# Prompt attention of a hybrid decoder step: score tiles of 1024 columns in place of 512

## The chip, the cores and the metric

The kernel runs on one NeuronCore of a Trainium2 chip. The metric is the device time of one execution in microseconds; the median of three runs before the change is 3355.91 us. The engines of the core that matter here are TensorE (PE in the profile, its weight loads PEld), VectorE (DVE), ScalarE (ACT) and GpSimd (POOL). Each of them works through its own queue in order.

## The reference, cut to what matters

The whole computation is one inference step of a one-layer decoder: an input projection, forgetting attention over a prompt of 2048 tokens with 8 heads of 64, an mLSTM over the same prompt, attention of 8 sample sequences over paged caches of 8192 keys each, an output projection with layer norm and an MLP with layer norm. The change lies in the attention over the prompt:

```python
SEQ, FOX_HEADS, FOX_HEAD_DIM, Q_BLOCK = 2048, 8, 64, 128

def _fox_prompt(q, k, v, logf):
    L = jnp.cumsum(logf, axis=1).transpose(0, 2, 1)
    ...
    def block(args):
        q_i, L_i, i = args
        s = jnp.einsum('bqhd,bkhd->bhqk', q_i, k).astype(jnp.float32) * scale
        s = s + L_i[..., :, None] - L[:, :, None, :]
        q_pos = i * Q_BLOCK + jnp.arange(Q_BLOCK)
        s = jnp.where(k_pos[None, :] <= q_pos[:, None], s, -jnp.inf)
        p = jax.nn.softmax(s, axis=-1)
        return jnp.einsum('bhqk,bkhd->bqhd', p.astype(v.dtype), v)
```

A row of scores belongs to one query. The mask is causal, so the 128 queries of row tile `qt` (0 to 15) see `(qt + 1) * 128` keys.

## The kernel before, in words

The kernel is one stream of instructions in program order, which a scheduler turns, at compile time, into one order for each engine. An instruction that comes earlier in the program goes first when its operands and its buffers are there; where they are not, a later one may pass it in the order that is compiled. On the chip the orders are fixed, and semaphores hold each engine until what it needs is done. A tile of a pool has a number of buffers (`bufs`); a new one can be written when the last reader of the tile that had its buffer before is through.

The stages are: input projections with the mLSTM beside them and the first part of the sample attention between them (up to about 940 us of the profiled span), the attention over the prompt (`phase_b`, about 940 to 1378 us), and then the output projection, the MLP and the rest of the sample attention, interleaved.

In `phase_b` the work is cut into 64 units, `units = [(h, g) ...]`: head `h` from 0 to 7, and within it `g` from 0 to 7. Unit `g` covers two row tiles of 128 queries, `qt = 2g` (called A below) and `qt = 2g + 1` (called B). The loop at the end of `phase_b` writes `scores` of unit n, then now and then `keys` and `queries` for what comes next, then `values` of unit n - 1 (`LA = 1`).

`scores(z, g)`: for A and then for B, the keys are taken in blocks of up to 512. Two matmuls (L1046 and L1047, query high part and low part) put a block of scores into a PSUM tile `pS`; there are three such banks, two of the stage's own and one that is shared. VectorE then adds the forget values (L1053; L1057 for the 128 columns at the diagonal, with the mask in `nd`), writes the sum into an SBUF tile `S` and keeps the row maximum of the block in `mx`. L1060 reduces these to the negative row maximum. `S` has 10 buffers of 512 columns of fp32.

`values(z, g, sc)`: for A and B, ScalarE takes the exponential of each `S` tile in place, with the row maximum as bias, and leaves the row sum of the tile in a column of `lp` (L1072: an ACTIVATE and then a read of the accumulator). L1073 adds up the columns of `lp`. Then, for chunks of four key blocks of 128 (`k0` = 0, 4, 8, 12) and in each for A and then B, TensorE transposes four 128x128 blocks of `S` into a PSUM tile `pt` of three buffers (L1085), ScalarE (L1088) or VectorE (L1090, for B's even chunks) copies it to `PT`, and TensorE multiplies the chunk with the values (L1094) into `po`. The chunks are called A0, B0, A1, B1, A2, B2, A3, B3 below. An `S` tile of 512 columns is read for the last time by the transposes of its one chunk.

At the end of a unit L1100 and L1102 move `po` to `ot`, and each fourth unit `finish` scales by the row sums and stores. `keys` (L1002, L149, L152) and `queries` (L149, L152) prepare the operands of the matmuls; `split_hi` (L149) and `split_lo` (L152) are helpers used all over the kernel.

Of the kernel before, what the change touches and what calls it, by code (L numbers as in the profile page):

```python
# [10 lines left out]
F32 = mybir.dt.float32  # L11
# [14 lines left out]
S = 2048  # L26
# [26 lines left out]
def body(ctx, tc, I, O, stages):  # L53
    nc = tc.nc
    V, A, G, T, SY = nc.vector, nc.scalar, nc.gpsimd, nc.tensor, nc.sync
# [20 lines left out]
    ident = cst.tile([128, 128], F32, name="ident")  # L76
# [52 lines left out]
    def tick(us):  # L129

        macc[0] += us
        while macc[1] and macc[0] > macc[2]:
            macc[0] -= macc[2]
            if beside(macc[1][0]) == 0:
                macc[1].pop(0)
        if not macc[1]:
            macc[0] = 0.0
        acc[0] += us
        while acc[1] is not None and acc[0] > acc[2]:
            acc[0] -= acc[2]  # L140
            attend()
# [809 lines left out]
    def phase_b():  # L951
        es = ExitStack()
        pb = es.enter_context(tc.tile_pool(name="pb", bufs=1, reuse_waits="tile"))
# [6 lines left out]
        def bank():  # L960

            turn[0] += 1
            if turn[0] % 3 == 0:
                return pps.tile([128, 512], F32, name="pS", tag="sX", bufs=1)
            return ppb.tile([128, 512], F32, name="pS", bufs=2)
# [61 lines left out]
        def scores(z, g):  # L1027

            qh, ql = z.pop(("q", g))
            ks = z["ks"]  # L1030
            forget = lambda a, b: Bz["nl"][:, a:b] if z["h"] == 0 and a < 512 else z["nl"][:, a:b]
            out = []
            for i in range(2):
                qt = 2 * g + i
                n = (qt + 1) * 128
                qs = slice(i * 128, i * 128 + 128)
                mx = pb.tile([128, 8], F32, name="mx", bufs=8)
                nd = pb.tile([128, 128], F32, name="nd", bufs=3)
                lastnd[0] = G.tensor_tensor(nd, forget(qt * 128, n), dmask, op=OP.add)
                st = []  # L1040
                j = 0
                for a in range(0, n, 512):
                    b = min(n, a + 512)
                    w = max(b - a, 256)
                    pS = bank()
                    T.matmul(pS[:, :w], qh[:, qs], ks[:, a:a + w], start=True, stop=False)  # L1046
                    last["PE"] = T.matmul(pS[:, :w], ql[:, qs], ks[:, a:a + w], start=False, stop=True)  # L1047
                    tick(0.42)
                    sp = pb.tile([128, 512], F32, name="S", bufs=10)
                    st.append(sp)  # L1050
                    e = min(b, qt * 128)
                    if e > a:
                        last["DVE"] = V.tensor_tensor_reduce(out=sp[:, :e - a], in0=pS[:, :e - a], in1=forget(a, e), scale=1.0, scalar=NEG,  # L1053
                                               op0=OP.add, op1=OP.max, accum_out=mx[:, j:j + 1])
                        j += 1
                    if b == n:
                        V.tensor_tensor_reduce(out=sp[:, e - a:b - a], in0=pS[:, e - a:b - a], in1=nd, scale=1.0, scalar=NEG,  # L1057
                                               op0=OP.add, op1=OP.max, accum_out=mx[:, j:j + 1])
                        j += 1
                V.tensor_reduce(mx[:, 7:8], mx[:, :j], axis=AX.X, op=OP.max, negate=True)  # L1060
                out.append((st, mx))
            return out

        def values(z, g, sc):

            for i, (st, mx) in enumerate(sc):
                qt = 2 * g + i
                n = (qt + 1) * 128
                lp = pb.tile([128, 4], F32, name="lp", bufs=8)
                for k, sp in enumerate(st):  # L1070
                    w = min(512, n - k * 512)
                    last["ACT"] = A.activation(sp[:, :w], sp[:, :w], AF.Exp, bias=mx[:, 7:8], accum_out=lp[:, k:k + 1])  # L1072
                V.tensor_reduce(z["ls"][:, qt:qt + 1], lp[:, :len(st)], axis=AX.X, op=OP.add)  # L1073

            po = ppb.tile([128, 256], F32, name="po", bufs=1)
            nk = 2 * g + 2
            for k0 in range(0, nk, 4):
                PT = pb.tile([128, 4, 256], F32, name="PT", bufs=4)
                for i in range(2):
                    kk = min(4, 2 * g + i + 1 - k0)  # L1080
                    if kk <= 0:
                        continue
                    pt = ppb.tile([128, 4, 128], F32, name="pt", bufs=3)
                    for k in range(kk):
                        T.transpose(pt[:, k], sc[i][0][k0 // 4][:, k * 128:(k + 1) * 128], ident)  # L1085
                    dst = PT[:, :kk, i * 128:i * 128 + 128]
                    if i == 0 or (k0 // 4) % 2 != 0:
                        A.copy(dst, pt[:, :kk])  # L1088
                    else:
                        V.tensor_copy(dst, pt[:, :kk])  # L1090
                for k in range(k0, min(k0 + 4, nk)):
                    q0 = 128 if k == nk - 1 else 0
                    c = (k % 2) * 64
                    last["PE"] = T.matmul(po[c:c + 64, q0:], z["vn"][:, k], PT[:, k - k0, q0:],  # L1094
                                          start=(k < 2), stop=(k >= nk - 2), skip_group_check=True)
                tick(0.45 * min(4, nk - k0))
            if g % 4 == 0:
                z["ot"] = pb.tile([64, 1024], F32, name="ot", bufs=2)
            od = z["ot"][:, (g % 4) * 256:(g % 4) * 256 + 256]
            A.copy(od, po[0:64])  # L1100
            q0 = 128 if g == 0 else 0
            V.tensor_tensor(od[:, q0:], od[:, q0:], po[64:128, q0:], op=OP.add)  # L1102
            if g % 4 == 3:
                finish(z, g // 4)

        def finish(z, half):

            h, ls, ot = z["h"], z["ls"], z["ot"]
            lr = pb.tile([128, 32], F32, name="lr", bufs=2)
            V.reciprocal(lr, ls)  # L1110
            lt = pb.tile([128, 32], F32, name="lt", bufs=2)
            V.transpose(lt, lr)
            o = half * 1024
            for a in range(4):
                SY.dma_start(drl[h, o:o + 1024].rearrange("(t a q) -> a t q", a=4, q=32)[a], lt[a * 32 + half * 8:a * 32 + half * 8 + 8])
            for q in range(2):
                rl = pb.tile([64, 512], F32, name="rl", bufs=2)
                SY.dma_start(rl, dap(drl, h * S + o + q * 512, [[0, 64], [1, 512]]))
                s = slice(q * 512, (q + 1) * 512)
                G.tensor_tensor(ot[:, s], ot[:, s], rl, op=OP.mult)  # L1120
                SY.dma_start(dmix[h // 2, (h % 2) * 64:(h % 2) * 64 + 64, o + q * 512:o + q * 512 + 512], ot[:, s])
# [12 lines left out]
        sc = {}  # L1134
        LA = 1
        for n in range(len(units) + LA):
            if 10 <= n < 16 and acc[1] is not None:

                with tc.issue_after(lastnd[0].ins):
                    attend()  # L1140
            if n == 12:
                wo.extend(half_wo(0, q) for q in range(4))
            if n < len(units):
                h, g = units[n]
                sc[n] = scores(Z[h], g)
                if h == 0 and g % 2 == 0 and g < 6:
                    keys(Z[0], g // 2 + 1)
                if h < 7:
                    if g == 3:
                        Z[h + 1] = head(h + 1)  # L1150
                        forget_values(Z[h + 1], 0, S)
                    if g >= 4:
                        keys(Z[h + 1], g - 4)
                if n + 1 < len(units):
                    queries(Z[units[n + 1][0]], units[n + 1][1])
            if n >= LA:
                h, g = units[n - LA]
                values(Z[h], g, sc.pop(n - LA))
# [698 lines left out]
```

## Time and profile before

| what | value |
|---|---|
| median of 3 runs | 3355.91 us (3352.63 to 3362.21) |
| profiled execution: span from first to last instruction | 3381.2 us (no other time is listed for it) |
| instructions | 57759 |
| mean granted TensorE clock | 0.988 of full speed |
| busy: PE, PEld | 3266.7 us (97%), 2623.4 us (78%) |
| busy: DVE, ACT, POOL | 2145.9 us (63%), 1413.8 us (42%), 869.5 us (26%) |
| attention over the prompt: exponentials, first and last start | 320, from 940.0 us to 1372.4 us |

How to read it: a busy share over the whole span is a mean over stages with different limits, so the stage from 940 to 1378 us is asked for by itself. A busy PE is not PE at its peak, because matmuls are pipelined and their ends are modelled; the waits of PE and of its weight loads say more. In a row of a group of instructions stand the line, the engine, the operation, the tiles written and read, the shape, the count, then the busy time and the mean length of one in ns, then the time that the engine stood idle just before them and what ended it. In a row of the timeline stand the start in us, the length in us, the engine, the line and the operation; several like instructions in a row are one row with their count.

### The profile page before, as it was taken

To read this page: it belongs to the slowest core of one execution; us is meant where nothing else is said; L and a number is where in the kernel's file an instruction comes from. 1 tells how busy PE (TensorE), PEld (TensorE's weight loads), DVE (VectorE), ACT (ScalarE), POOL (GpSimd) and SP (SyncE) were. 2 spreads that over 40 slices of the span, in tenths; PEclk is the share of its full clock that TensorE was granted. 3 is DMA by queue.
4 is the path that set the end of the run, shared out by engine and by line. 5 is a ranking of instruction groups with operands and counts; after the bars stand their busy time and mean duration, and the time that the engine had idled before them with its cause. 6 is when DMAs were issued, how large, how long until landed. Compare 5 with 4: busy or idle time off the path is not lost. (4 is left out here: it accounts for less than half of the span.)

```text
span 3381.2 us, 57759 instructions
## 1 busy us (share of the span) xinstructions
PE 3266.7 (97%) x21564; PEld 2623.4 (78%) x21564; DVE 2145.9 (63%) x5180; ACT 1413.8 (42%) x2989; POOL 869.5 (26%) x928
## 2 busy tenths in 40 slices
PE   9999999999999999999999999999999999999998
PEld 8998897787866667677777776777777777888886
DVE  5857567556478878655666667666676545644545
ACT  4444245334378888422332333232332323433332
POOL 0112122422332222365423324323243110100001
PEclk9999999999999999999999999999999999999999
DMA  5665765866652322587776768767678545532221
GB/s 172 165 189 179 221 206 180 292 212 219 227 166 81 90 76 61 209 283 245 286 249 244 247 226 299 254 234 270 209 258 289 198 164 160 168 103 83 87 76 66
DMA packets 427232, 646.25 MB, mean 191 GB/s; under 512 B 83148, under 2 KB 320016, under 8 KB 426056
## 3 DMA queue, kind: packets, MB, share of 16 engines
q1 hardware_dynamic: 350184, 363.22, 35.3%
q0 software_dynamic: 74304, 270.57, 21.8%
q10 hardware_dynamic: 2464, 8.78, 0.7%
q8 instruction: 170, 2.79, 0.3%
q14 instruction: 110, 0.90, 0.1%
HBM read 589.63 MB, written 52.83 MB: 190 GB/s over the span
## 5 line engine op out<-in xcount | busy, mean ns | idle before, releaser
L1422 DVE TENSOR_TENSOR y<-y,py 128x512 f32<-128x512 f32 (+1 forms) x475 | 320.5, 681 | 310.7 <-PE py L159 287.4
L149 ACT ACTIVATE wh<-wr 128x1024 fp32r<-128x1024 f32 x268 | 278.1, 1056 | 500.8 <-PE py L159 215.3
L159 PE MATMUL ph<-x1h,wl 128*128 128x512 f32 (+1 forms) x1280 | 452.9, 355 | 7.7 <-DVE wl L152 7.1
L157 PE MATMUL ph<-x1h,wh 128*128 128x512 f32 (+1 forms) x1280 | 454.9, 355 | 3.6 <-ACT wh L149 2.9
L1597 POOL DMA_INDIRECT kT<-cache_k,idxK x256 | 272.5, 1064 | 718.2 <-PE sQ L1626 657.7
L158 PE MATMUL ph<-x1l,wh 128*128 128x512 f32 (+1 forms) x1280 | 454.4, 355 | 0.0
L1603 DVE STREAM_TRANSPOSE kT<-kT 128x512 f32<-128x512 f32 x512 | 330.3, 685 | 177.1 <-DMA kT<-cache_k,idxK 170.5
L157 PE MATMUL py<-wh,hh 128*128 128x512 f32 (+1 forms) x1088 | 431.7, 399 | 6.8 <-DVE y L1420 4.0
L158 PE MATMUL py<-wl,hh 128*128 128x512 f32 (+1 forms) x1088 | 426.4, 392 | 0.6 <-issue 0.6
L159 PE MATMUL py<-wh,hl 128*128 128x512 f32 (+1 forms) x1088 | 426.3, 393 | 0.3 <-issue 0.3
L152 DVE TENSOR_TENSOR wl<-wr,wh 128x1024 fp32r<-128x1024 f32 x268 | 335.0, 1256 | 81.5 <-ACT wh L149 28.6
L157 PE MATMUL pm<-whi,xhT 128*128 128x256 f32 (+2 forms) x1088 | 319.0, 293 | 4.6 <-ACT whi L149 1.7
L158 PE MATMUL pm<-wlo,xhT 128*128 128x256 f32 (+2 forms) x1088 | 313.8, 289 | 0.8 <-DVE wlo L152 0.8
L159 PE MATMUL pm<-whi,xlT 128*128 128x256 f32 (+3 forms) x1088 | 313.5, 288 | 0.0
L157 PEld LDWEIGHTS ph<-x1h,wh 128*128 128x128 f32 x1280 | 241.8, 189 | 42.9 <-issue 5.2
L159 PEld LDWEIGHTS ph<-x1h,wl 128*128 128x128 f32 x1280 | 241.8, 189 | 43.0 <-DVE wl L152 9.4
L158 PEld LDWEIGHTS ph<-x1l,wh 128*128 128x128 f32 x1280 | 241.9, 189 | 36.9 <-issue 4.1
L157 PEld LDWEIGHTS py<-wh,hh 128*128 128x128 f32 (+1 forms) x1088 | 201.3, 185 | 64.4 <-issue 11.9
L159 PEld LDWEIGHTS py<-wh,hl 128*128 128x128 f32 (+1 forms) x1088 | 200.9, 185 | 52.7 <-issue 5.3
L158 PEld LDWEIGHTS py<-wl,hh 128*128 128x128 f32 (+1 forms) x1088 | 201.4, 185 | 40.6 <-issue 2.3
L157 PEld LDWEIGHTS pm<-whi,xhT 128*128 128x128 f32 (+1 forms) x1088 | 207.9, 191 | 13.7 <-issue 7.8
L1072 ACT ACTIVATE S<-S,mx 128x512 f32<-128x512 f32 (+2 forms) x320 | 207.8, 652 | 17.7 <-DVE mx L1060 16.6
(394 smaller groups left out, 6534.9 us busy)
## 6 DMA issues: line engine op xcount, KB each, us to landing
wr<-w SPq DMA_DIRECT2D x256, 512.0 KB
wra<-w_in SPq DMA_DIRECT2D x112, 512.0 KB
Rb<-dR SPq DMA_DIRECT2D x128, 128.0 KB
wr<-w_o SPq DMA_DIRECT2D x16, 512.0 KB
xr<-dmix SPq DMA_DIRECT2D x16, 512.0 KB
y<-x_prompt SPq DMA_DIRECT2D x16, 512.0 KB
dx<-y SPq DMA_DIRECT2D x16, 512.0 KB
xr<-dx SPq DMA_DIRECT2D x16, 512.0 KB
```

The source lines that it names most:

```text
L149: last["ACT"] = A.activation(dst, src, AF.Copy, scale=scale)
L152: r = (eng or V).tensor_tensor(dst, src, hi.bitcast(F32), op=OP.subtract)
L157: T.matmul(ps, wh, xh, start=first, stop=False)
L158: T.matmul(ps, wh, xl, start=False, stop=False)
L159: last["PE"] = T.matmul(ps, wl, xh, start=False, stop=stop)
L1072: last["ACT"] = A.activation(sp[:, :w], sp[:, :w], AF.Exp, bias=mx[:, 7:8], accum_out=lp[:, k:k + 1])
L1422: V.tensor_tensor(y, y, ps, op=OP.add)
L1597: G.indirect_dma_start(out=piece(n), out_offset=None, in_=ck, in_offset=IO(ap=idxK[:, b, j // 2, j % 2:j % 2 + 1], axis=0))
L1603: V.transpose(x, x)
```

## The change

Each `S` tile becomes 1024 columns wide and there are 5 of them in place of 10 of 512, so the memory is the same. Two blocks of 512 scores, each still with its own matmuls, PSUM bank and sums, go into the two halves of one `S` tile. One exponential then covers up to 1024 columns, with one read of its row sum, and the transposes pick their block out of the wider tile. Nothing else is changed.

```diff
--- before
+++ after
@@ scores, in the loop over blocks of 512 keys
                     tick(0.42)
-                    sp = pb.tile([128, 512], F32, name="S", bufs=10)
-                    st.append(sp)
+                    if a % 1024 == 0:
+                        st.append(pb.tile([128, 1024], F32, name="S", bufs=5))
+                    sp = st[-1][:, a % 1024:a % 1024 + 512]
                     e = min(b, qt * 128)
@@ values
                 for k, sp in enumerate(st):
-                    w = min(512, n - k * 512)
+                    w = min(1024, n - k * 1024)
                     last["ACT"] = A.activation(sp[:, :w], sp[:, :w], AF.Exp, bias=mx[:, 7:8], accum_out=lp[:, k:k + 1])
                 V.tensor_reduce(z["ls"][:, qt:qt + 1], lp[:, :len(st)], axis=AX.X, op=OP.add)
@@ values, transposes
                     for k in range(kk):
-                        T.transpose(pt[:, k], sc[i][0][k0 // 4][:, k * 128:(k + 1) * 128], ident)
+                        T.transpose(pt[:, k], sc[i][0][k0 // 8][:, (k0 % 8 + k) * 128:(k0 % 8 + k + 1) * 128], ident)
```

## The prediction

> **What bounds the kernel now.** I read the page first, for the length and for where the exponentials lie.
>
> ```profile
> span 3381.2 us, 57759 instructions
> ...
> ACT  4444245334378888422332333232332323433332
> ...
> L1072 ACT ACTIVATE S<-S,mx 128x512 f32<-128x512 f32 (+2 forms) x320 | 207.8, 652 | 17.7 <-DVE mx L1060 16.6
> ```
>
> The ACT line is the span in 40 slices of 84.5 us; the stretch of 7s and 8s is the prompt attention, and the 320 exponentials of L1072 are busy 207.8 us in it, the dearest single thing that ScalarE does there. So the next view is busy time by stretches: the stage, then one whole head (head 3, 1102.1 to 1156.0 us), then two stretches of it in which the values of units 4 and 5 and the scores of units 5 and 6 are made.
>
> ```profile
> core 0: us, PE busy (x) PEld busy (x) DVE busy (x) ACT busy (x) POOL busy (x), PEclk, DMA share, GB/s
> 940.00:1378.00 438.00, 431.38 (x2984) 300.32 (x2986) 345.12 (x1369) 363.74 (x1020) 120.19 (x198) 0.99 0.32 90
> 1102.10:1156.00 53.90, 53.81 (x378) 37.38 (x377) 43.22 (x172) 45.83 (x129) 14.89 (x25) 1.00 0.28 79
> 1130.10:1138.30 8.20, 8.20 (x59) 5.44 (x58) 5.52 (x20) 6.15 (x18) 2.76 (x5) 1.00 0.26 62
> 1138.30:1147.00 8.70, 8.70 (x64) 6.35 (x62) 6.97 (x24) 7.84 (x22) 1.32 (x3) 1.00 0.10 24
> ```
>
> In the stage ACT is busy 363.74 of 438.00 us (83%), DVE 345.12 (79%), PE 431.38 (98%). In one head PE is busy 53.81 of 53.90 us. A modelled busy time could hide that PE starves, so I asked the view of waits for PE in the stage (what waited, for what; us in total, times, longest), and the groups of instructions of head 3 for its weight loads, which stall first.
>
> ```profile
> engine line waited for: us in total, times, longest us
> PE pS L1046 <- ACT qh L149: 3.3, 1, 3.3
> PE po L1094 <- DVE ot L1102: 0.9, 1, 0.9
> PE pt L1002 <- POOL dup L981: 0.7, 1, 0.7
> PE po L1094 <- DVE ls L1073: 0.7, 1, 0.7
> PE pt L1085 <- DVE PT L1090: 0.4, 1, 0.4
> ```
>
> ```profile
> L1085 PEld LDWEIGHTS pt<-ident,S 128*128 128x128 f32 x137 | 16.1, 140 | 8.0 <-issue 3.8 <-ACT PT L1088 0.8 <-ACT S L1072 0.4
> ...
> L1094 PEld LDWEIGHTS po<-PT,vn 128*64 128x64 f32 x144 | 8.8, 136 | 6.9 <-issue 1.9 <-DVE PT L1090 0.7 <-ACT PT L1088 0.4
> ```
>
> The PE waits add up to 3.3 + 0.9 + 0.7 + 0.7 + 0.4 = 6.0 us in 438, none of them for an exponential; the largest is one wait for queries at the start. The weight loads of head 3 stood idle 8.0 + 6.9 us, but the largest share of those gaps ended with "issue" (3.8 and 1.9), which is no wait for data; ScalarE ended 0.8 + 0.4 + 0.4 = 1.6 us of them, and the exponentials 0.4 us alone. So TensorE is the bound of this stage, at its own pace. ScalarE and VectorE have slack, and what they wait for is not each other only:
>
> ```profile
> DVE S L1053 <- PE pt L1085: 26.2, 50, 2.7
> ```
>
> Fifty times VectorE stood still until transposes had read an old `S` tile. The ten `S` buffers are full most of the time: the scores run ahead as far as they have buffers. That is the resource that the change makes coarser.
>
> **The change, part by part.** All later sums draw on the timeline of unit 7's start in head 3. The transposes are those of unit 6 (x4 at 1153.24 is its B2, x1 its A3, x2 its B3) and of unit 7 (x4 at 1157.28 is A0, x4 at 1158.61 is B0).
>
> ```profile
> 1152.53 0.69 DVE L1053 CUSTOM_DVE_ANT_0 S<-pS,nl 128x512 f32<-128x512 f32 x1
> ...
> 1153.14 0.09 DVE L1053 DVE_READ_ACCUMULATOR2_ANT mx<- 128x1 f32 x1
> ...
> 1153.24 0.66 PE L1085 MATMUL pt<-ident,S 128*128 128x128 f32 x4
> ...
> 1153.65 0.48 PE L1046 MATMUL pS<-ks,qh 128*128 128x512 f32 x1
> ...
> 1153.97 0.40 PE L1047 MATMUL pS<-ks,ql 128*128 128x512 f32 x1
> ...
> 1154.54 0.55 DVE L1053 CUSTOM_DVE_ANT_0 S<-pS,nl 128x384 f32<-128x384 f32 x1
> ...
> 1155.01 0.29 DVE L1057 CUSTOM_DVE_ANT_0 S<-pS,nd 128x128 f32<-128x128 f32 x1
> ...
> 1155.31 0.33 PE L1085 MATMUL pt<-ident,S 128*128 128x128 f32 x1
> ...
> 1155.34 0.16 DVE L1060 TENSOR_REDUCE mx<-mx 128x1 f32<-128x5 f32 x1
> ...
> 1155.84 0.72 ACT L1072 ACTIVATE S<-S,mx 128x512 f32<-128x512 f32 x1
> ...
> 1155.96 0.38 PE L1085 MATMUL pt<-ident,S 128*128 128x128 f32 x2
> ...
> 1156.27 1.08 PE L1094 MATMUL po<-PT,vn 128*64 128x256 f32 x8
> ...
> 1157.26 0.71 ACT L1072 ACTIVATE S<-S,mx 128x512 f32<-128x512 f32 x1
> ...
> 1157.28 0.66 PE L1085 MATMUL pt<-ident,S 128*128 128x128 f32 x4
> ...
> 1157.69 0.42 PE L1046 MATMUL pS<-ks,qh 128*128 128x384 f32 x1
> ...
> 1157.97 0.71 ACT L1072 ACTIVATE S<-S,mx 128x512 f32<-128x512 f32 x1
> 1158.13 0.40 PE L1046 MATMUL pS<-ks,qh 128*128 128x512 f32 x1
> ...
> 1158.37 0.40 PE L1047 MATMUL pS<-ks,ql 128*128 128x512 f32 x1
> ...
> 1158.61 0.60 PE L1085 MATMUL pt<-ident,S 128*128 128x128 f32 x4
> ...
> 1159.24 0.40 ACT L1072 ACTIVATE S<-S,mx 128x128 f32<-128x128 f32 x1
> ...
> 1159.63 0.50 ACT L1072 ACTIVATE S<-S,mx 128x256 f32<-128x256 f32 x1
> ```
>
> *Fewer exponentials.* A head has 4 x (1 + 2 + 3 + 4) = 40 tiles of 512 columns and will have 8 x 1 + 8 x 2 = 24 of 1024, so 16 exponentials and 16 reads of the sum go per head, 128 in all. From start to start a 512 one with its read takes 1157.97 - 1157.26 = 0.71 us and a 128 one 1159.63 - 1159.24 = 0.39, so 128 columns cost (0.71 - 0.39) / 3 = 0.107 and one of 1024 columns should take 0.71 + 4 x 0.107 = 1.14 us. Each merge saves 0.71 + 0.71 - 1.14 = 0.28 us, 128 of them 36 us of ScalarE. No 1024 exponential is in the trace: between no fixed part saved (1.42 us each, nothing won) and free extra columns (0.71) lie 0 and 91 us; the line through the two rows is the nearest thing and I take 36.
>
> What this is worth to the end is what TensorE waits for ScalarE: 1.6 us a head at most, 13 us for eight, and 0.4 x 8 = 3 us for exponentials alone. Much of a gap in the weight loads lies under running matmuls. I take -2 us, bounds -13 and 0. The cover is TensorE's own work; if that were gone, the 36 us would show.
>
> *Shorter sum of the row sums.* L1073 reduces 2 columns in place of up to 4, with the same count of instructions: nothing, under VectorE's 21% slack. The index arithmetic of the transposes issues the same instructions: nothing. No DMA is added, removed or moved.
>
> *Coarser buffers.* An `S` buffer of 512 columns came free after one chunk of transposes. One of 1024 comes free after its second chunk, and the order of chunks is A0, B0, A1, B1, A2, B2, A3, B3: at unit 7 the first comes free after A1, then after B1, A3 and B3. Unit 7 needs four buffers and unit 6 holds four of five. So of unit 7 the first half of A goes into the fifth, the second half waits for A1 of unit 6, B's first half for B1, and B's second half for A3. Before, B's last block waited for B2 (the sum at 1154.54 follows it). In small units 0 to 4 the new scores also come some microseconds later, but their exponentials lie well ahead of the transposes in this trace (unit 0's 128-column exponential at 1159.24 belongs to a unit whose transposes come after all eight chunks of unit 7), so I count nothing there.
>
> The price at unit 7: A3 ends at 1155.31 + 0.33 = 1155.64. Then on VectorE a 512 block, 1153.14 - 1152.53 = 0.61; the 384 block, 1155.01 - 1154.54 = 0.47; the diagonal, 1155.34 - 1155.01 = 0.33; the maximum, 0.16; then the exponential, 1.14. That is 2.71 us, so B0 could start at 1158.35, with hand-overs of 0.1 to 0.6 us (maximum to exponential took 1155.84 - 1155.50 = 0.34 here) between 1158.45 and 1158.95. It starts at 1158.61 now. But the trace covers the time from 1157.69 to 1158.61 with scores of units 0 and 1 of the next head, and these have no buffer then: unit 0's A gets the one of B3, its B waits for A1 of unit 7. TensorE can still put them into the three PSUM banks, as far as B's second half has left them. So TensorE runs dry for between 0 (the banks take it all) and 1158.95 - 1157.69 = 1.3 us. Behind the waiting VectorE instruction stand its copies to `PT`, which TensorE needs too. I take 0.75 us a head, a little over the middle, since both the chain and the cover get worse: +6 us for eight heads, bounds 0 and +10.
>
> At units 5 and 6 the last buffer comes free after A2, and the chain is one 512 block shorter, 0.61. The two stretches shown have 8.20 - 5.52 = 2.68 and 8.70 - 6.97 = 1.73 us of idle VectorE, into which the bunched blocks fit. I take 0; the upper bound is 1.3 - 0.61 = 0.7 us at each, 16 x 0.7 = +11 us.
>
> A rule of the Trainium skill weighs here. Perfetto Trace Analysis, section Optimizing Scalar/DVE Operations, says that grouping helps where the engine is saturated, and that where it is not, but makes bubbles elsewhere, breaking instructions up may let work end sooner. This case's 83% is the unsaturated side. By it alone the merge would be a loss of 1.14 - 0.71 = 0.43 us for the first chunks of A and B in each unit 7, 16 x 0.43 = 7 us and 3363; it is the same delay that my chain holds already, so I do not add it.
>
> *Pairs of scores.* Room now comes for two blocks at a time. A score pair that follows transposes takes 1153.97 - 1153.65 = 0.32 us to its second matmul, one that follows another score 1158.37 - 1158.13 = 0.24. If all 16 merges a head made such a neighbour, 128 x 0.08 = 10 us would be won. But a PSUM bank still comes free one at a time, so I take -1, bounds -10 and 0. Other interleaving may also change the "issue" gaps between kinds of matmul, 3.8 + 1.9 us a head; a tenth of them either way is 5 us, value 0.
>
> Sum: -2 + 0 + 6 + 0 - 1 + 0 = +3 us. The profiled execution spans 3381.2 us and the page lists no time around it; the median of the timed runs is 3355.91, 25 us less, and I take the difference over to it unscaled (a per cent of 3 us is nothing): 3359 us. About 0.3%, 10 us, is what a measurement of this kernel can tell from no change (its three runs spread over 9.6 us).
>
> **The rivals.**
>
> *TensorE starves at the ends of the heads (slower).* The mechanism is the one above, the wait of B's last scores for A3, at its upper price: it decides from the point where B0's exponential ends more than 1157.69 - 1155.64 = 2.05 us after A3 and the banks hold nothing for TensorE to do. Then unit 7 costs 10 us and units 5 and 6 11 us: +21, 3377 us. For it speak the 50 waits of 26.2 us for `S` buffers with ten of them already; against it that TensorE never waited for an exponential though the lead is short there now. Chance 0.33.
>
> *ScalarE holds the stage (faster).* If the modelled PE times hide waits, the 1.6 us a head go whole and the pairs come in part: -13 us and, with a part of the pairs, 3340 to 3343 us. Fully bound by ScalarE it would be 3356 - 36 = 3320. For it speaks ACT's 83%; against it the idle weight loads, which name ScalarE in a tenth of their gaps. Chance 0.10, nearly all of it near 3343. The Trainium skill, Perfetto Trace Analysis, section Identifying the Most-Contended Engine, tells to judge TensorE by its weight-load share and not by matmul busy time: here that is 300.32 of 438.00, 69%, which would make ScalarE the most contended engine and 3320 the answer. The trace bears it out badly so far, for the reason given; it is worth 0.02 of that 0.10.
>
> *The change saves no ScalarE time.* If a 1024 exponential took 1.42 us, the chain at unit 7 would be 0.28 longer, 8 x 0.28 = 2 us, and the 2 us gained would go: 3363. Against it stands the straight line of the two rows. Chance 0.02.
>
> **How the numbers follow.** Forecast, 3359 within 10 us of before: 0.55. With the last rival 0.57 end inside 0.3%. But 3359 has +7 to the edge and -13, so I move 0.01 to the slower side: faster 0.10, same 0.56, slower 0.34. The range: below, 3356 - 13 = 3343, rounded to 3344; above, 3377 and some of the 5 us of issue gaps, 3380. The likeliest case's own range is 3350 to 3366.
>
> **What would show it.** In the profile after: 192 exponentials with a mean near 0.9 us (24 a head for 136 x 128 columns, so 725 columns each: 0.40 + (725 - 128) / 128 x 0.107), ACT busy in the stage about 36 us less, TensorE's length of the stage nearly unchanged (438 us, +3); VectorE's waits for transposes before L1053 well over 26 us; small new gaps of TensorE or its weight loads that end with an exponential, at B0 of unit 7 in each head. It is wrong if the stage shortens by over 10 us (then ScalarE's time was on the path), or if PE shows repeated gaps of over 1 us at units 5 to 7 (then the buffers decide).

## The result, and the profile after

The changed kernel takes 3365.29 us (median of 20 runs) against 3357.50 us (20 runs) before: ratio 1.0025, 95% interval 1.0015 to 1.0035, so 8 us slower, between 5 and 12. The prediction was 3359 us, +3 us, in a range of 3344 to 3380.

The first view is that of the tile `S`: each row has the range of durations in ns, then the start of the first and of the last instruction of the group. Before, and then after:

```profile
L1085 PE MATMUL pt<-ident,S x1088: 270/272/421, 941.7 to 1377.6; 128*128 128x128 f32 x182
L1072 ACT ACTIVATE S<-S,mx x320: 386/709/741, 940.0 to 1372.4; 128x512 f32<-128x512 f32 x128, 128x128 f32<-128x128 f32 x16, 128x384 f32<-128x384 f32 x16
```

```profile
L1086 PE MATMUL pt<-ident,S x1088: 270/273/421, 931.3 to 1378.7; 128*128 128x128 f32 x182
...
L1073 ACT ACTIVATE S<-S,mx x192: 385/982/1164, 929.5 to 1373.1; 128x1024 f32<-128x1024 f32 x80, 128x128 f32<-128x128 f32 x16, 128x256 f32<-128x256 f32 x16, 128x384 f32<-128x384 f32 x16
```

There are 192 exponentials in place of 320, as written. From the first to the last transpose of `S` the stage takes 1377.6 - 941.7 = 435.9 us before and 1378.7 - 931.3 = 447.4 after: 11.5 us more, at the upper end of the timed interval. This length, read from the same two instructions in every kernel, is the measure in the experiments. (It leaves out only the stage's first scores and the work behind the last transpose. The whole profiled executions are not compared: the one before spans 3381.2 us, longer than any of its timed runs, of which the longest is 3365.84; the one after spans 3368.8.)

The lengths are not quite at the same clock. Over the 25 us from the first transpose on, the granted clock was 0.86 before and 0.93 after, so the length before holds some 25 x 0.07 = 1.8 us (an estimate) that the order of the work has no part in. The steady heads, 2 to 6, ran at a granted clock of 1.00. From the first transpose of one head to that of the next they take 53.9 us before and 55.7 after on the mean: 1.8 us a head more, 14 us if all eight were alike.

Busy time of the stage after, and the groups of exponentials by shape:

```profile
929.00:1379.00 450.00, 441.66 (x2987) 303.06 (x2987) 346.53 (x1372) 331.30 (x763) 117.63 (x198) 1.00 0.31 88
```

```profile
L1073 ACT ACTIVATE S<-S,mx 128x1024 f32<-128x1024 f32 x80 | 91.8, 1148 | 32.9 <-DVE mx L1061 31.9 <-DVE ls L1074 0.6 <-ACT PT L1089 0.2
...
L1073 ACT ACTIVATE S<-S,mx 128x512 f32<-128x512 f32 x16 | 11.5, 717 | 0.4 <-DVE mx L1061 0.4
...
L1073 ACT ACTIVATE S<-S,mx 128x128 f32<-128x128 f32 x16 | 6.3, 394 | 2.0 <-DVE mx L1061 2.0
```

ScalarE is busy 331.30 of 450 us; it was 363.74 of 438. So it did lose 32 us, and it stands idle for 119 us in place of 74. A 1024 exponential lasts 1148 ns, one of 512 columns 717 and one of 128 394. TensorE's waits after, over the stretch from first to last transpose:

```profile
PE pS L1046 <- ACT qh L149: 3.0, 1, 3.0
PE pt L1086 <- DVE ls L1074: 2.8, 8, 0.3
...
PE pt L1086 <- ACT S L1073: 0.6, 2, 0.4
```

TensorE itself waited for exponentials 0.6 us, twice, and eight times 0.3 us, once a head, for a VectorE row (below). So the 11.5 us are not there. The gaps before its weight loads say more, once two kinds are kept apart. Five rows of the timeline of weight loads before, in head 3:

```profile
1152.22 0.63 PEld L1094 LDWEIGHTS po<-PT,vn 128*64 128x64 f32 x8 [0.17 <-DVE mx L1060]
1153.24 0.42 PEld L1085 LDWEIGHTS pt<-ident,S 128*128 128x128 f32 x4 [0.39 <-issue]
...
1154.29 0.63 PEld L1094 LDWEIGHTS po<-PT,vn 128*64 128x64 f32 x8 [0.37 <-ACT PT L1088]
1155.31 0.14 PEld L1085 LDWEIGHTS pt<-ident,S 128*128 128x128 f32 x1 [0.39 <-issue]
...
1156.26 0.20 PEld L1094 LDWEIGHTS po<-PT,vn 128*64 128x64 f32 x4 [0.17 <-issue]
```

Where TensorE goes over to the value matmuls (L1094) its weight load stands idle 0.17 us behind transposes and 0.37 behind scores, and where it leaves them 0.39 us (medians over the stage before: 0.168 us of 60 such gaps, 0.364 of 64, and 0.384 of 104 from value matmuls to transposes). The length is the same whether the gap is put down to "issue", to VectorE or to ScalarE: it is the price of the change of kind, and the releaser beside it is no cause. Only gaps elsewhere, or beyond these lengths, are waits for data. Sorted so from all weight-load rows between the first and the last transpose (us of idle weight loads; a burst is a run of value matmuls with nothing between; gaps under 0.15 us, which the views do not list, are left out of the waits):

```
                          bursts   changes of kind   waits   length
before                       131              81.4    11.5    435.9
after                        147              90.9    17.2    447.4
```

So the change made 16 more bursts and 5.7 us more of waits. A burst costs TensorE about 0.24 us. From its first start to the next kind's, a burst of 8 takes 1157.28 - 1156.27 = 1.01 us (rows of the prediction) and one of 4 takes 1153.33 - 1152.75 = 0.58 (rows of unit 7 below): 0.108 a matmul and 0.15 for the burst itself. The instruction ahead of it takes 0.09 more to the next start than otherwise (medians of heads 2 to 6: 202 ns in place of 109 for a transpose, 326 in place of 232 for a score). 16 x 0.24 = 3.8, and 3.8 + 5.7 = 9.5 of the 11.5 us; the rest is not accounted for. One of the new places is where scores come right behind a burst, in the view of waits of the weight loads, before and after:

```profile
PEld pS L1046 <- issue: 0.8, 2, 0.4
```

```profile
PEld pS L1046 <- issue: 14.0, 37, 0.4
```

Three of VectorE's waits, before and then after:

```profile
DVE S L1053 <- PE pt L1085: 26.2, 50, 2.7
DVE S L1053 <- PE pS L1047: 14.4, 17, 1.2
...
DVE PT L1090 <- PE pt L1085: 7.6, 9, 2.0
```

```profile
DVE PT L1091 <- PE pt L1086: 36.2, 41, 2.7
DVE S L1054 <- PE pS L1047: 27.4, 40, 1.0
DVE ls L1074 <- ACT S L1073: 11.3, 15, 1.3
DVE S L1054 <- PE pt L1086: 7.9, 7, 1.1
```

It waits for old `S` tiles less than before (7.9 us, it was 26.2) and more for transposes that it has to copy (36.2 us, it was 7.6) and for scores (27.4 us, it was 14.4).

Unit 7's start in head 3, from the timeline after: the x1 at 1149.27 is A3 of unit 6, the x4 at 1151.93 A0 of unit 7, the x8 at 1154.24 B0 and A1, the x8 at 1155.63 B1 and A2.

```profile
1149.27 0.33 PE L1086 MATMUL pt<-ident,S 128*128 128x128 f32 x1
...
1149.36 0.49 PE L1046 MATMUL pS<-ks,qh 128*128 128x512 f32 x1
...
1149.68 0.39 PE L1047 MATMUL pS<-ks,ql 128*128 128x512 f32 x1
...
1150.11 0.69 DVE L1054 CUSTOM_DVE_ANT_0 S<-pS,nl 128x512 f32<-128x512 f32 x1 [0.54 <-PE pS L1047]
...
1151.93 0.66 PE L1086 MATMUL pt<-ident,S 128*128 128x128 f32 x4
...
1151.96 0.27 DVE L1061 TENSOR_REDUCE mx<-mx 128x1 f32<-128x5 f32 x2
1152.21 1.15 ACT L1073 ACTIVATE S<-S,mx 128x1024 f32<-128x1024 f32 x1 [1.05 <-DVE mx L1061]
...
1152.75 0.65 PE L1095 MATMUL po<-PT,vn 128*64 128x256 f32 x4
...
1153.33 0.19 PEld L1046 LDWEIGHTS pS<-ks,qh 128*128 128x128 f32 x1 [0.38 <-issue]
1153.33 0.44 PE L1046 MATMUL pS<-ks,qh 128*128 128x384 f32 x1
1153.36 1.14 ACT L1073 ACTIVATE S<-S,mx 128x1024 f32<-128x1024 f32 x1
...
1154.24 1.03 PE L1086 MATMUL pt<-ident,S 128*128 128x128 f32 x8
...
1154.49 0.56 ACT L1089 COPY PT<-pt 128x512 f32<-128x512 f32 x1
1154.88 0.69 DVE L1091 COPY PT<-pt 128x512 f32<-128x512 f32 x1 [2.65 <-PE pt L1086]
...
1155.49 0.14 DVE L1074 TENSOR_REDUCE ls<-lp 128x1 f32<-128x2 f32 x1
...
1155.62 0.86 PEld L1086 LDWEIGHTS pt<-ident,S 128*128 128x128 f32 x8 [0.58 <-DVE ls L1074]
1155.63 1.09 PE L1086 MATMUL pt<-ident,S 128*128 128x128 f32 x8 [0.35 <-DVE ls L1074]
```

B's second half has its first scores only at 1149.36, after A3 began, its sum at 1150.11, its maximum with the two reductions of 1151.96, and B's exponential at 1152.21. B0 follows without a wait. The two exponentials of 1.15 us stand in ScalarE's queue ahead of the copy of A0, whose transposes were through at 1152.59 and which is copied at 1154.49. TensorE then stands 0.35 us before B1 (its weight loads 0.58, which is 4.7 of the waits in eight heads). But that wait ends with VectorE and not with ScalarE. VectorE waited 2.65 us for the transposes of B0 and copied them until 1154.88 + 0.69 = 1155.57, and L1074, to which the profile puts the wait down, comes right behind the copy. In the first head the weight loads' gap of 0.58 us at the same place (988.52 us) is put down to this copy, L1091, itself. That B1 needs the PSUM bank that the copy of B0 empties is read from this order, not shown.

### The profile page after: what moved, and what is told of

Its sections match the earlier page's. It is cut to its first block, busy times and chain, and to the rows that moved or that the text cites. A ratio compares the mean times of both kernels' runs of the same rounds, so it can differ in the third digit from the quotient of the medians.

```text
span 3368.8 us, 57553 instructions
## 1 busy us (share of the span) xinstructions
PE 3262.5 (97%) x21564; PEld 2618.8 (78%) x21564; DVE 2149.7 (64%) x5180; ACT 1382.0 (41%) x2733; POOL 866.7 (26%) x928
## 5 line engine op out<-in xcount | busy, mean ns | idle before, releaser
L1715 POOL DMA_INDIRECT vt<-cache_v,idxV x158 | 162.3, 1027 | 193.9 <-PE sO L1739 139.8
```

Of the source, the lines that this page charges most:

```text
L1715: G.indirect_dma_start(out=vt.rearrange("p f c -> p (f c)"), out_offset=None, in_=cv, in_offset=IO(ap=idxV[:, b, (kt % 4) * 4 + kt // 4, f ...
```

## The experiments

Two theories and a third that would make both idle. G: the room in `S` decides; tiles that come free late, two chunks at a time, hold the scores back, and TensorE gets a worse order or starves. L: the long exponential decides; what is behind it on ScalarE comes late. R: the scheduler only landed on another order by chance. Ratios are against the kernel before on the same chip, with 95% intervals. The row under each is the transposes' row of its `S` view, from which the length is read; it is 435.9 us before and 447.4 after the change. The steady head is 53.9 us before and 55.7 after.

### Wide tiles, exponentials of 512

```diff
-                for k, sp in enumerate(st):
-                    w = min(1024, n - k * 1024)
+                for k in range((n + 511) // 512):
+                    w = min(512, n - k * 512)
+                    sp = st[k // 2][:, k % 2 * 512:k % 2 * 512 + w]
...
```

> Tiles of 1024 columns, five of them, but the exponential again in pieces of 512 with a sum each (320 of them). Theory G (the coarse release of the buffers makes the compiled order on TensorE dearer and holds the scores back): nothing comes back, and ScalarE's 36 us are spent again: steady head 55.7 us or a little more, ratio to before 1.0025 or above. Theory L (the long exponential does it: copies to PT and first chunks queue behind 1.14 us pieces on ScalarE): steady head near 53.9 us, ratio 1.000. Theory R (the scheduler merely landed on another order, good or bad by chance): the pairs of kinds in this kernel's compiled order, priced by the starts in the two traces, give 0.75 us a head less than the changed kernel; with no stall that is near 54 us.

```profile
L1087 PE MATMUL pt<-ident,S x1088: 270/273/421, 926.3 to 1374.8; 128*128 128x128 f32 x182
```

Measured: ratio 1.0037 (1.0024 to 1.0050), length 448.5 us, steady head 55.6 us. TensorE's waits in this kernel (who, for what; total us, times, longest):

```profile
PE pt L1087 <- ACT PT L1090: 3.8, 9, 0.5
PE pt L1087 <- DVE PT L1092: 3.5, 8, 0.4
...
PE po L1096 <- ACT PT L1090: 2.0, 7, 0.3
```

With the exponentials short again the whole loss stays, so L falls. R's price of the order was right in itself (126 bursts, 21 fewer than after the change and five fewer than before), but the time did not follow it: here TensorE waits, 3.8 + 3.5 + 2.0 us for copies, and the waits of its weight loads, sorted as above, are 24.8 us in place of 11.5. The comparison with the changed kernel also says what the merge by itself is worth: 448.5 - 447.4 = 1.1 us for 32 us of ScalarE. The steady heads give nothing (55.6 against 55.7) and the timed ratios 0.12%, 4 us, with intervals that overlap; the two orders differ too, so no more can be said than that it is worth little.

### Six wide tiles

```diff
-                        st.append(pb.tile([128, 1024], F32, name="S", bufs=5))
+                        st.append(pb.tile([128, 1024], F32, name="S", bufs=6))
...
-            n = pb.tile([128, t, 2, 64], F32, name="dup", tag=f"dup{t}", bufs=3)
+            n = pb.tile([128, t, 2, 64], F32, name="dup", tag=f"dup{t}", bufs=2)
```

> The changed kernel with six S tiles of 1024 in place of five; the room comes from the tile dup, which gets two buffers in place of three. Theory G: the sixth buffer lets unit 7's third half-row in earlier and all the small units of the next head, steady head 53.9 us or less, ratio 1.000 or below. Theory L: the exponentials are as long as before, steady head stays near 55.7, ratio 1.0025. Theory R: the order's price is 0.95 us a head below the changed kernel's, 54 to 55 us by its stalls.

```profile
L1086 PE MATMUL pt<-ident,S x1088: 270/272/421, 936.7 to 1373.7; 128*128 128x128 f32 x182
```

Measured: ratio 1.0002 (0.9990 to 1.0013), length 437.0 us, steady head 54.3 us. One more tile brings back 10.4 of the 11.5 us, with the exponentials as long as in the changed kernel: 121 bursts and 13.2 us of waits. `dup` was changed with it, so that this alone would say little; the next two say it again.

### Five wide tiles, freed earlier

```diff
-            for k0 in range(0, nk, 4):
-                PT = pb.tile([128, 4, 256], F32, name="PT", bufs=4)
+            for c0 in range(0, nk, 8):
+                ks_ = range(c0, min(c0 + 8, nk), 4)
+                PTs = {k0: pb.tile([128, 4, 256], F32, name="PT", bufs=4) for k0 in ks_}
...
                 for i in range(2):
+                    for k0 in ks_:
...
+                        if i == 1:
+                            weigh(k0)
```

`weigh` holds the value matmuls of one chunk.

> The changed kernel with the chunks in the order A0 A1 B0 B1 A2 A3 B2 B3, so that an S tile of 1024 comes free after the second, fourth, sixth and eighth chunk in place of the third, fourth, seventh and eighth. Theory G: about half of the loss comes back or more, steady head 54 to 55 us, ratio 1.000 to 1.0015. Theory L: no change, 55.7 us. Theory R: the order's price is 1.25 us a head below the changed kernel's, so 54 us and a ratio of 1.000 or below.

```profile
L1098 PE MATMUL pt<-ident,S x1088: 270/273/421, 929.9 to 1364.9; 128*128 128x128 f32 x182
```

Measured: ratio 0.9994 (0.9979 to 1.0008), length 435.0 us, steady head 53.7 us. With the same five tiles, only the order of the chunks is changed, and with it which chunk frees which tile, and all of the loss is gone (110 bursts, 17.8 us of waits). By their forecasts this experiment and the one before it do not part G from R: R had 54 to 55 and then 54 us a head, against 54.3 and 53.7 measured, and G had 53.9 or less and then 54 to 55. The first, the fourth and the fifth do.

### Eight narrow tiles

```diff
-                    sp = pb.tile([128, 512], F32, name="S", bufs=10)
+                    sp = pb.tile([128, 512], F32, name="S", bufs=8)
```

> The kernel before with eight S tiles of 512 in place of ten: the look-ahead shrinks by a fifth, the release stays fine and the exponentials stay short. Theory G (amount of buffer room is what the order lives from): steady head 55 us or more, ratio above 1.001. Theory L: 53.9 us, ratio 1.000. Theory R: the order's price is 0.3 us a head below that of the kernel before, so 53.6 to 54 us unless it stalls.

```profile
L1085 PE MATMUL pt<-ident,S x1088: 270/272/421, 934.0 to 1378.7; 128*128 128x128 f32 x182
```

Measured: ratio 1.0024 (1.0014 to 1.0035), length 444.7 us, steady head 55.4 us. The loss of the changed kernel appears in the kernel before, with its short exponentials, when a fifth of its room is taken away. VectorE's and TensorE's longest waits in this kernel:

```profile
DVE S L1053 <- PE pt L1085: 34.8, 42, 1.9
```

```profile
PE pS L1046 <- DVE mx L1057: 4.4, 13, 0.5
```

VectorE waits 34.8 us for transposes to free a tile (26.2 with ten), and TensorE waits in turn for VectorE, 4.4 us in this row. The waits of its weight loads, sorted as above, are 28.2 us, some 12 of them ended by VectorE, with 112 bursts.

### Four wide tiles

```diff
-                        st.append(pb.tile([128, 1024], F32, name="S", bufs=5))
+                        st.append(pb.tile([128, 1024], F32, name="S", bufs=4))
```

> The changed kernel with four S tiles of 1024 in place of five, so that a unit of four has no buffer until the one before it lets go. Theory G (TensorE starves for lack of S room): unit 7 can begin only after chunk A1 of unit 6; steady head 57 to 61 us, ratio 1.005 to 1.014. If only the compiled order counted (theory R): its pair price equals the changed kernel's, 55.7 us, ratio 1.0025.

```profile
L1086 PE MATMUL pt<-ident,S x1088: 270/273/421, 925.9 to 1402.9; 128*128 128x128 f32 x182
```

```profile
PE pt L1086 <- ACT S L1073: 28.2, 26, 1.6
```

Measured: ratio 1.0145 (1.0124 to 1.0166), length 477.0 us, steady head 59.3 us. R expected the changed kernel's time, since the order's price was the same; it is 29.6 us more, and one row holds 28.2 us, TensorE waiting for exponentials. Of these waits 9.8 us stand before B0 of unit 7, and 11.1 and 6.9 before B0 of units 5 and 6, once in every head. That is the slower rival of the prediction (10 us at unit 7, 11 at units 5 and 6), in its place and rather above its size, with one tile less than the change has. The ratio lies just above G's 1.005 to 1.014.

### The new chunk order with narrow tiles

The kernel before, with the third experiment's edit of the loop over chunks and no other:

```diff
-            for k0 in range(0, nk, 4):
+            for c0 in range(0, nk, 8):
...
                 for i in range(2):
+                    for k0 in ks_:
...
+                        if i == 1:
+                            weigh(k0)
```

> The kernel before (ten S tiles of 512) with the chunk order A0 A1 B0 B1 A2 A3 B2 B3 of the third experiment. Theory G: here each chunk frees its tile at once in either order, so nothing is to be won by release: steady head 53.6 to 54.3 us, ratio 0.999 to 1.0015. If the new chunk order is better by itself (fewer bursts of value matmuls): 52 to 53 us, ratio near 0.997, and the third experiment would say little on release.

```profile
L1097 PE MATMUL pt<-ident,S x1088: 270/272/421, 927.8 to 1363.4; 128*128 128x128 f32 x182
```

Measured: ratio 1.0017 (1.0006 to 1.0029), length 435.6 us, steady head 54.3 us. The chunk order is no gain by itself, so what it gave back with wide tiles was release. The length is that of the kernel before, yet the timed runs are 0.17% slower, 5.7 us. Some 3 us of this are in the heads, 54.27 - 53.92 = 0.35 us in each steady one, which the lower clock at the start of the profile before hides in the length. Where the rest lies was not found.

### Both repairs

The third experiment's edit with the second's six tiles; against the third:

```diff
-                        st.append(pb.tile([128, 1024], F32, name="S", bufs=5))
+                        st.append(pb.tile([128, 1024], F32, name="S", bufs=6))
...
-            n = pb.tile([128, t, 2, 64], F32, name="dup", tag=f"dup{t}", bufs=3)
+            n = pb.tile([128, t, 2, 64], F32, name="dup", tag=f"dup{t}", bufs=2)
```

> The changed kernel with both repairs, the chunk order of the third experiment and the six tiles of the second. Theory G: the two ease the same shortage, so they add up in part only: steady head 53.2 to 53.8 us, ratio 0.998 to 0.9995. If they were independent gains of 2.0 and 1.4 us a head: 52.3 us, ratio 0.996.

```profile
L1098 PE MATMUL pt<-ident,S x1088: 270/273/421, 923.6 to 1359.2; 128*128 128x128 f32 x182
```

Measured: ratio 1.0005 (0.9992 to 1.0019), length 435.6 us, steady head 53.7 us. The two do not add up: either is enough, and then TensorE's own work is left.

### Twelve narrow tiles

```diff
-                    sp = pb.tile([128, 512], F32, name="S", bufs=10)
+                    sp = pb.tile([128, 512], F32, name="S", bufs=12)
...
-            n = pb.tile([128, t, 2, 64], F32, name="dup", tag=f"dup{t}", bufs=3)
+            n = pb.tile([128, t, 2, 64], F32, name="dup", tag=f"dup{t}", bufs=2)
```

> The kernel before with twelve S tiles of 512 (dup has two buffers in place of three). Theory G: TensorE stalled little with ten, so there is little left: steady head 53.3 to 53.9 us, ratio 0.9985 to 1.000. If room still bound it at ten: 52.5 us or less, ratio 0.9965.

```profile
L1085 PE MATMUL pt<-ident,S x1088: 270/272/421, 926.3 to 1360.6; 128*128 128x128 f32 x182
```

Measured: ratio 1.0004 (0.9990 to 1.0019), length 434.3 us, steady head 53.9 us. Room did not bind at ten.

### Fewer bursts of value matmuls

The kernel before with twelve tiles and the new chunk order, where the value matmuls of two chunks are written together behind their transposes; against the sixth experiment, beside the twelve tiles:

```diff
-                        if i == 1:
-                            weigh(k0)
+                for k0 in ks_:
+                    weigh(k0)
```

> An attempt at a version that beats both: twelve S tiles of 512 (dup has two buffers), the chunk order A0 A1 B0 B1, and the value matmuls of two chunks written together after their transposes. The compiled order has 11 bursts of value matmuls a head in place of 17 before and 14.4 in the eighth kernel. If the gaps between kinds of matmul (issue, some 0.37 us each) bind where room is plenty: 3 to 6 bursts less a head are 1 to 2 us a head, from first to last transpose 422 to 429 us, ratio 0.996 to 0.998. If the longer bursts only make TensorE wait for copies to PT instead: 434 to 440 us, ratio 0.999 to 1.002.

```profile
L1097 PE MATMUL pt<-ident,S x1088: 270/272/421, 928.9 to 1367.3; 128*128 128x128 f32 x182
```

```profile
PEld pS L1046 <- DVE mx L1053: 16.1, 43, 1.2
```

Measured: ratio 1.0026 (1.0013 to 1.0038), length 438.4 us, steady head 54.4 us. The bursts are 92, 39 fewer than before, worth 39 x 0.24 = 9 us; but the waits are 28.4 us in place of 11.5, about half of them scores that wait for VectorE (16.1 us of gaps in one row, fixed ones among them). The length fits the second expectation, but the copies to `PT` that it named are not the main wait. One was bought with the other, and no version was found that beats the kernel before.

With 0.24 us a burst and the waits, the length of each kernel comes out of the kernel before's, in us:

```
                    bursts  waits   0.24 x bursts + waits   measured
                                    against before
the change             147   17.2                    +9.5      +11.5
split exponentials     126   24.8                   +12.1      +12.6
six wide               121   13.2                    -0.7       +1.1
five, freed earlier    110   17.8                    +1.3       -0.9
eight narrow           112   28.2                   +12.1       +8.8
four wide              149   52.1                   +44.9      +41.1
new order, narrow      108   17.8                    +0.8       -0.3
both repairs           125   11.8                    -1.1       -0.3
twelve narrow          115   15.8                    +0.5       -1.6
fewer bursts            92   28.4                    +7.5       +2.5
```

It is an account after the fact, good to some 5 us, and the signs of the small differences are not in it; but it has the sign and the size of each of the four that lost more than 5.

## Why the prediction was right, and where its steps were not

**The size.** The forecast of +3 us had the direction, but it lies below what was measured, 5 to 12 us; the measured 3365 us lies inside the range, at the upper edge of what was given for the likeliest case, 3350 to 3366. In the list of signs, the 192 exponentials came with a mean of 0.90 us as forecast and ScalarE's busy time fell by 32 us (36), but the stage, which was to stay nearly as long (+3), grew by 11.5.

**What bounds the stage.** TensorE at its own pace: right. ScalarE lost 32 us (forecast 36; the 1024 exponential took 1153.36 - 1152.21 = 1.15 us from start to start, forecast 1.14), and by the first experiment that was worth some 1 us (forecast 2). The faster rival fell with it. The Trainium skill, Perfetto Trace Analysis, section Identifying the Most-Contended Engine, would have one judge TensorE by its weight-load share, beside its matmul throughput, which was not worked out here; the share was 69% before, is 303.06 of 450.00 = 67% after, and pointed to ScalarE. Here the measurement differs: the waits and gaps of TensorE named the bound, the share did not.

**Coarser buffers.** The mechanism was right: the same 5120 columns of room make a stage of 435.9 us in ten pieces, 447.4 in five, and 435.0 in five that are freed in a better order. The same page, section Optimization Strategy, says that a gap that repeats on the engine that should be saturated can mean too little SBUF for the next tile. The experiment with four tiles bears that out: 28.2 us of gaps, nearly all before B0 of units 5 to 7 in every head, where five tiles have 0.6 us in that row.

**Its price and its place.** For waits +6 us were counted at unit 7, and the waits grew by 5.7, 4.7 of them at unit 7. But they stand at B1 and not at B0: the compiled order had put enough other work before B0, and what TensorE stood still for was VectorE, behind its copy of B0. So the step that has TensorE run dry at B0, at the end of the chain of sums and exponential, did not happen with five tiles, and that the +6 fits the 5.7 is in part luck.

**Other interleaving** is the term that was mis-sized: it was set at 0, with 5 us either way, and came out at +3.8 by the bursts. The prediction took it to be as likely good as bad. The runs show that a shortage of room costs 9 to 13 us here in three kernels (the changed one, the first experiment, the fourth), while its split into bursts (147, 126, 112) and waits (17.2, 24.8, 28.2 us) differs from order to order. With this term the sum of +3 is +6.8. The timed runs say +8, but the profiled stage grew by 11.5, so that the sum comes so near is in part luck too.

**The gaps put down to ScalarE**, 1.6 us a head, which bounded the gain: most of them were the fixed gaps of a change of kind. Over the whole stage before, 12.2 us of gaps end with ScalarE's copies or exponentials, and 1.2 us of these are left when the fixed gaps are taken off. So the bound of 13 us was too wide and the 2 us taken nearly right.

**Small units and units 5 and 6.** Nothing was counted there for waits, and 4.7 of the 5.7 us lie at unit 7: right, as far as waits go.

**Pairs of scores.** A head of the trace (heads 2 to 6) has 16 scores that follow another in place of 8, so more pairs came than the -1 us was for. But the 0.08 us that was to be won by each is not there: in the steady heads before, a transpose ahead of a score goes over to it after 28 ns, where it takes 109 to another transpose, so the longer way to the second matmul (316 ns in place of 236) is paid back ahead of it. By these rows the term is nothing, and not because of the PSUM banks.

**What would show it.** That VectorE's waits for old tiles would rise well over 26 us was wrong: they fell to 7.9, while its waits for scores and for transposes to copy rose. A wait that a shortage makes is not always found at the instruction that lacks the room.

**The slower rival**, +21 us, was the right mechanism one tile too early: the fifth experiment is it.

## What to carry to other kernels

Equal bytes are not equal room: a pool of half as many tiles, twice as wide, frees them later, and the length of the stage follows the last reader of each tile. Look in which order the chunks of a tile are read for the last time before buying memory; here a reordering was worth as much as a sixth tile. And an engine at 83% that hardly anybody waits for repays little: 32 us of ScalarE bought some 1 us.

## What the runs showed of the hardware that was not expected

Each change between the value matmuls and any other kind leaves the weight loads idle for a fixed time, 0.39 us on leaving and 0.17 or 0.37 on entering, whatever releaser the profile puts beside it. A burst cost about 0.24 us of TensorE, 131 times in this stage before the change. In the sixth and ninth experiments the timed runs were slower by more than the stage's length explains (1.0017 with 435.6 us, 1.0026 with 438.4). Their steady heads (54.3 and 54.4 us, against 53.9) explain a part of it; the cause of the rest stays open.
